# Sample states of a hybrid decoder layer: the first decay factor taken out of the scores, the outgoing prompt state in two slots, the values' rows in half tiles, and HGRN2's factors copied at level 64

## The chip, the cores and the metric

The kernel runs on one core of a Trainium2 chip. The core has a matrix engine (TensorE, PE in the profile; its weight loads are PEld), a vector engine (VectorE, DVE), a scalar engine (ScalarE, ACT), a general engine (GpSimd, POOL) and a sync engine (SyncE, SP) that issues most DMA transfers. Each engine works through its own instructions in order. The metric is the device time of one execution in microseconds (us), lower is better.

## The reference, cut to what matters

One inference step of one decoder layer for 256 + 16 prompt tokens and 8 sample tokens: a half-step FFN, a mixer, a second half-step FFN, with 2048 channels. The mixer is one projection of 2048 to 20480 channels, then 8 heads of retention (256 x 256 states) and 16 heads of HGRN2 (128 x 128 states) side by side, a gated merge and one output projection. A sample token updates a stored state of its own in each head and reads it:

```python
# retention, one sample token (C = 1): gamma is a constant of the head
S_new = gamma * S + k^T v                 # k_dec = k
o = (q k^T) v + (gamma * q) S             # q_dec = q * gamma
# HGRN2, one sample token: f is a vector of 128 factors, k = 1 - f
S_new = f[:, None] * S + k^T v
o = (q k^T) v + (q * f) S
...
def decoder_layer(x, pos, s_ret, s_hg, prompt, ...):
    x = layer_norm(ALPHA * x + 0.5 * swiglu(x, f1_g, f1_u, f1_d), ln1_g, ln1_b)
    m, s_ret, s_hg = token_mixer(x, pos, s_ret, s_hg, prompt, w_in, lb, hg_norm_g, w_out)
    x = layer_norm(ALPHA * x + m, ln2_g, ln2_b)
    x = layer_norm(ALPHA * x + 0.5 * swiglu(x, f2_g, f2_u, f2_d), ln3_g, ln3_b)
    return x, s_ret, s_hg
```

The outputs are the tokens and all states, those of the prompt and those of the samples (8 samples x 8 heads x 256 x 256 and 8 x 16 x 128 x 128 numbers).

## The kernel before, in words

All tokens stand side by side in the free dimension (280 columns, 264 where the meta tokens aren't needed), channels on the partitions. Every dense product is made in three passes, with the operands split into a high and a low part: `xh` by `whi`, `xl` by `whi`, `xh` by `wlo`. The weights stream through in units of 512 KB (eight 128 x 128 blocks): SP loads `raw` (L184), ACT casts it to `whi` (L187), DVE subtracts to get `wlo` (L188), PE does 24 matmuls (L217). There are three buffers of each.

PE's order is written out by hand in the program. The projection runs head by head (`pj_q_r`, `pj_k_r`, `pj_v_r`, `pj_q_h`, `pj_f`, `pj_i_h`; then the gates `pj_g_r`, `pj_a_r`, `pj_g_h`, `pj_a_h` of the head before), and the mixers are generators that are advanced by a few steps after each slice of the projection: a `yield n` in them says after how many such steps they go on. The order on ACT, DVE, POOL and SP is made by the tile scheduler from this program; on the chip it is fixed.

`mix_ret` is one retention head `u`. It splits keys and values (`ks`, `vs`), computes the scores of the prompt (`psc`) and multiplies them with a decay table into `dtab`'s tile (`scr`), and computes the outgoing prompt state in two halves `psr`, each copied by ACT into a tile with the tag `sro` (L1051) and written out (`out_srp`, L1052). The sample states come in four tiles `smr` (128 x 4 x 256: one half of the key channels, four samples each; L988). ACT multiplies a whole tile by the head's constant, which POOL has put in a small tile `gam` (L1062, L1067); then DVE adds key times values' row for each sample (L1070). For that the values' rows of the samples are written to a scratch (`vrd`, L720) and read back spread over all partitions into `vbr` (L1038). `gam` shares the one slot of the tag `sro` with the outgoing state:

```python
gam = tmp("sro", (P, 1))
nc.gpsimd.memset(gam, GAMMA[u])
```

The new states go out (`out_srs`, L1073), and 32 small matmuls `pqr` read them (L1084), after the prompt's four small matmuls at L1025. `vbr` is one buffer of 4 x 256 numbers a partition, so its second spread (samples 4 to 7) waits for the last update of samples 0 to 3.

`mix_hg` is the two HGRN2 heads of the same `u`. It works through levels of doubling length (2, 4, ... 64, 128): `scale_k` and `scale_q` multiply keys and queries in place by a level's decay, from the tile of the tag `T2`, `T4`, ... `T64`. Its sample states `smh` (16 heads x 8 samples) are scaled one sample at a time by ACT, with the sample's factors `fk[:, 0]` (L906), and updated by DVE (L907), then written out (L910) and read by the matmuls `pq`.

Of the kernel before, what the change touches and what calls it, by code (L numbers as in the profile page):

```python
# [13 lines left out]
AF = mybir.ActivationFunctionType  # L14
ALU = mybir.AluOpType
# [3 lines left out]
P = 128  # L19
# [4 lines left out]
NMETA, SEQ, NS = 16, 256, 8  # L24
LP = NMETA + SEQ
# [28 lines left out]
GAMMA = [1.0 - 2.0 ** (-5.0 - h) for h in range(HR)]  # L54
# [73 lines left out]
def trunk(ctx: ExitStack, tc: tile.TileContext, A, O):  # L128
    nc = tc.nc
# [416 lines left out]
    with tc.tile_pool(name="yp", bufs=1) as yp:  # L546
# [7 lines left out]
        with tc.tile_pool(name="mp", bufs=1) as mp:  # L554

            rows = {n: (r if isinstance(r, list) else [r]) for n, r in {
# [3 lines left out]
            }.items()}  # L560

            def tmp(name, shape=(P, T), bufs=1, dt=F32, tag=None):
                if name in rows:
                    rows[name] = rows[name][1:] + rows[name][:1]
                    return rp.tile(list(shape), dt, tag=rows[name][-1], name=name)
                return mp.tile(list(shape), dt, tag=tag or name, name=name, bufs=bufs)
# [166 lines left out]
            def mix_hg(u, f, k, q, v):  # L733
# [11 lines left out]
                fk = tmp("fk", (P, 2, 2, NS))  # L745
# [4 lines left out]
                sms, vbs = [], []  # L750
# [78 lines left out]
                vrow = []  # L829
                for h in range(2):  # L830
# [4 lines left out]
                    x = pt[:64, 2 * P : 3 * P]  # L835
# [24 lines left out]
                for s in LEVELS[MASKED:]:  # L860
                    pl = mx_bank("pl")
                    for h in range(2):
                        for b in range(2):
                            k0, q0, o = NMETA + b * P, b * P, (2 * h + b) * s
                            if s == 64:
                                j = 64 * b
# [24 lines left out]
                Tt = Ts[2 * LEVELS[-1]]  # L891
                on = tmp("on_h", (P, 2, TL), bufs=2)
                on_h[u] = on
                kts = []
                for h in range(2):
                    kt = tmp("kth", (P, 2, P), bufs=2)
                    kts.append(kt)
                    pt = mx_bank("ptk")
                    for b, (t0, n) in enumerate(((NMETA, P), (NMETA + P, P), (0, NMETA))):
                        nc.tensor.transpose(pt[:n, b * P : (b + 1) * P], K[:, h, t0 : t0 + n], ident)  # L900
                    nc.scalar.copy(kt, pt[:, : 2 * P].rearrange("p (b f) -> p b f", b=2))
                    upper_upper_lower(km[:, h, :], pt[:NMETA, 2 * P : 3 * P])

                    vb, sm = vbs[h], sms[h]
                    for b in range(NS):
                        nc.scalar.activation(sm[:, b, :], sm[:, b, :], AF.Copy, scale=fk[:, 0, h, b : b + 1])  # L906
                        nc.vector.scalar_tensor_tensor(  # L907
                            out=sm[:, b, :], in0=vb[:, b, :], scalar=fk[:, 1, h, b : b + 1], in1=sm[:, b, :],
                            op0=ALU.mult, op1=ALU.add)
                    nc.sync.dma_start(O["sgs"][2 * u + h], sm)  # L910
                    yield 2
# [3 lines left out]
                for h in range(2):  # L915
# [7 lines left out]
                    for b in range(2):  # L923
                        nc.vector.scalar_tensor_tensor(
                            out=S[:, b + 1, :], in0=S[:, b, :], scalar=Tt[:, h, b : b + 1],
                            in1=pst[:, (b + 1) * P : (b + 2) * P], op0=ALU.mult, op1=ALU.add)
# [3 lines left out]
                for h in range(2):  # L930
                    for b in range(NS):
                        j = 32 * (b % 4)
# [45 lines left out]
            def mix_ret(u, q, k, v):  # L978
# [4 lines left out]
                sms = []  # L983
# [11 lines left out]
                for c in range(2):  # L995
# [12 lines left out]
                    for b, (t0, n) in enumerate(BLOCKS):  # L1008
                        x, g = pt[:n, b * P : (b + 1) * P], dec[:n, b, u : u + 1]
                        his = [ks[:, 0, b, f]] if b < 2 else [ks2[third[0], c, :], ks2[third[1], c, :]]  # L1010
                        for hi in his:
                            nc.scalar.activation(hi, x, AF.Copy, scale=g)
                        nc.vector.scalar_tensor_tensor(
                            out=(ks[:, 1, b, f] if b < 2 else ks2[third[2], c, :]), in0=x, scalar=g,
                            in1=his[0].bitcast(F32), op0=ALU.mult, op1=ALU.subtract)
# [15 lines left out]
                c2 = SCORES[2][0]  # L1031
                mul(scr[:, :c2], psc[:, :c2], dt[:, :c2])
                scrs = [scr[:, SCORES[0][0] : SCORES[1][0]], scr[:, SCORES[1][0] : c2], sc2]
                vbs = []

                def spread(e):
                    vbs.append(tmp("vbr", (P, 4, 256)))
                    nc.sync.dma_start(vbs[e], vrow[4 * e : 4 * e + 4, :].partition_broadcast(P))  # L1038

                spread(0)  # L1040
                yield 4

                for c in range(2):
# [14 lines left out]
                centre(vlast.unsqueeze(1))  # L1058
                upper_lower_upper(vs2.rearrange("p c f -> p (c f)"), vlast)

                gam = tmp("sro", (P, 1))
                nc.gpsimd.memset(gam, GAMMA[u])  # L1062
                for e in range(2):
                    vb = vbs[e]
                    for c in range(2):
                        sm = sms[2 * e + c]
                        nc.scalar.activation(sm, sm, AF.Copy, scale=gam)  # L1067
                        for j in range(4):
                            t = LP + 4 * e + j
                            nc.vector.scalar_tensor_tensor(  # L1070
                                out=sm[:, j, :], in0=vb[:, j, :], scalar=k[:, c, t : t + 1], in1=sm[:, j, :],
                                op0=ALU.mult, op1=ALU.add)
                        nc.sync.dma_start(O["srs"][u, c, :, 4 * e : 4 * e + 4, :], sm)  # L1073
                    if e == 0:
                        spread(1)
                    yield 1 + 5 * (1 - e)
                yield 15 + 2 * calm
                pq = mx_bank("pqr")
# [171 lines left out]
```

## Time and profile before

| | |
|---|---|
| median of 3 runs | 2607.2 us (2603.62 to 2609.99) |
| the profiled execution | 2608.29 us, of which 2606.2 us are the profile's span |
| granted PE clock in it | 0.997 of full speed |
| first FFN | 0 to about 790 us |
| the eight heads | about 790 to 1800 us |
| output projection and second FFN | about 1800 us to the end |
| w_in loads | 320 transfers of 512 KB, 4.5 us from issue to landing |
| sample states in / out (retention) | 32 / 32 transfers of 512 KB, 4.7 / 4.7 us |
| spreads of the values' rows | 16 transfers of 512 KB, 4.1 us |

A profile shows one execution. "A <- B" in a list of waits means that A sat idle until B was done. A row of a timeline has the start, the length, the engine, the line of the program, the operation, what it writes and reads, and in brackets the idle time of the engine just before it and what ended that. SPq is SP's queue of DMA issues: a row there is the issue, not the transfer.

### The profile page before, as it was taken

Reading aid. Unit: us, or ns where it says so; the run is one execution under the profiler, and the core shown is the slowest. Engines: PE = TensorE matmul, PEld = TensorE weight load, DVE = VectorE, ACT = ScalarE, POOL = GpSimd, SP = SyncE. Lnnn points to the kernel's source line nnn. Section 1 sums busy time; section 2 is a strip of 40 time slices with the busy share of each in tenths; the row PEclk is TensorE's granted clock in tenths of the full one; section 3 lists DMA queues with packets and bytes.
Section 4 is the critical chain, followed back from the end, with each engine's and each line's share of the span. In section 5 each row is a group of like instructions: output and inputs, shape, how many; then the busy total and the mean of one; then the engine's idle time right before and its main releaser. Section 6 shows DMA issues by size and latency. Waiting matters only on the chain.

```text
span 2606.2 us, 56106 instructions
## 1 busy us (share of the span) xinstructions
PE 2580.9 (99%) x23400; PEld 2546.5 (98%) x23400; DVE 1703.7 (65%) x2859; ACT 1375.4 (53%) x2160; POOL 13.7 (1%) x62
## 2 busy tenths in 40 slices
PE   9999999999999989999999999999999999999999
PEld 9999999999999889999999999999999999999998
DVE  6444454565579777777777777776995555556555
ACT  5444444444456566666666666665564444444444
POOL 0000000000000000000000000000000000000000
PEclk9999999999999999999999999999999999999999
DMA  7555555555566675767676767676656666666664
GB/s 240 184 183 185 186 185 182 184 186 185 182 200 223 216 269 183 265 207 260 210 258 210 256 206 263 203 235 194 193 187 201 195 195 195 195 197 193 197 197 147
DMA packets 154591, 536.25 MB, mean 206 GB/s; under 512 B 17696, under 2 KB 25696, under 8 KB 154336
## 3 DMA queue, kind: packets, MB, share of 16 engines
q1 hardware_dynamic: 154048, 532.37, 63.0%
q8 instruction: 183, 3.00, 0.5%
q14 instruction: 72, 0.59, 0.1%
q10 hardware_dynamic: 288, 0.29, 0.0%
HBM read 501.99 MB, written 30.61 MB: 204 GB/s over the span
## 4 chain that ended last, share of the span: by engine, by line
PE 92%; DVE 4%; DMA 2%; ACT 1%; issue 1%; SPq 0%; POOL 0%; ACTq 0%; POOLq 0%; DVEq 0%
PE up L217 35%; PE dn L217 18%; PE pj_f L217 4%; PE pj_q_h L217 3%; PE wo L217 3%; PE pj_k_r L217 3%; PE pj_v_r L217 3%; PE pj_g_r L217 3%; PE pj_i_h L217 3%; PE pj_q_r L217 3%; PE pj_a_r L217 3%; PE pj_g_h L217 3%; PE pj_a_h L217 3%; DVE wlo L188 2%; DMA vbr<-vrd 1%; PE pqr L1084 1%
## 5 line engine op out<-in xcount | busy, mean ns | idle before, releaser
L188 DVE TENSOR_TENSOR wlo<-raw,whi 128x1024 fp32r<-128x1024 f32 (+1 forms) x869 | 1062.4, 1223 | 748.6 <-ACT whi L187 745.4
L187 ACT CAST whi<-raw 128x1024 fp32r<-128x1024 f32 (+1 forms) x870 | 905.3, 1042 | 911.4 <-PE up L217 413.1
L217 PE MATMUL up<-xh,wlo 128*128 128x280 f32 (+1 forms) x2624 | 726.0, 280 | 1.3 <-DVE wlo L188 1.3
L217 PE MATMUL up<-xh,whi 128*128 128x280 f32 (+1 forms) x2624 | 725.7, 280 | 1.0 <-ACT whi L187 1.0
L217 PE MATMUL up<-xl,whi 128*128 128x280 f32 (+1 forms) x2624 | 725.4, 279 | 0.0
L217 PEld LDWEIGHTS up<-xh,wlo 128*128 128x128 f32 x2624 | 492.5, 189 | 2.3 <-DVE wlo L188 2.3
L217 PEld LDWEIGHTS up<-xh,whi 128*128 128x128 f32 x2624 | 492.6, 189 | 1.3 <-ACT whi L187 1.2
L217 PEld LDWEIGHTS up<-xl,whi 128*128 128x128 f32 x2624 | 492.6, 189 | 0.0
L217 PE MATMUL dn<-hh,whi 128*128 128x280 f32 (+1 forms) x1376 | 384.7, 280 | 0.0
L217 PE MATMUL dn<-hh,wlo 128*128 128x280 f32 (+1 forms) x1376 | 384.3, 279 | 0.0
L217 PE MATMUL dn<-hl,whi 128*128 128x280 f32 (+1 forms) x1376 | 384.3, 279 | 0.0
L217 PEld LDWEIGHTS dn<-hh,whi 128*128 128x128 f32 x1376 | 260.1, 189 | 0.1
L217 PEld LDWEIGHTS dn<-hl,whi 128*128 128x128 f32 x1376 | 260.1, 189 | 0.1
L217 PEld LDWEIGHTS dn<-hh,wlo 128*128 128x128 f32 x1376 | 260.1, 189 | 0.0
L217 PE MATMUL pj_g_r<-xh,whi 128*128 128x264 f32 x256 | 76.8, 300 | 0.0
L217 PE MATMUL pj_g_h<-xh,whi 128*128 128x264 f32 x256 | 73.7, 288 | 0.0
L217 PE MATMUL pj_k_r<-xh,whi 128*128 128x280 f32 x256 | 73.7, 288 | 0.0
L217 PE MATMUL pj_v_r<-xh,whi 128*128 128x280 f32 x256 | 73.5, 287 | 0.0
L217 PE MATMUL pj_v_r<-xh,wlo 128*128 128x280 f32 x256 | 72.4, 283 | 0.3 <-DVE wlo L188 0.3
L217 PE MATMUL pj_k_r<-xh,wlo 128*128 128x280 f32 x256 | 72.5, 283 | 0.0
L217 PE MATMUL pj_k_r<-xl,whi 128*128 128x280 f32 x256 | 72.3, 283 | 0.0
L217 PE MATMUL pj_v_r<-xl,whi 128*128 128x280 f32 x256 | 72.3, 283 | 0.0
(393 smaller groups left out, 5235.6 us busy)
## 6 DMA issues: line engine op xcount, KB each, us to landing
raw<-in_w_up SPq DMA_DIRECT2D x343, 512.0 KB, 4.2
raw<-in_w_in SPq DMA_DIRECT2D x320, 512.0 KB, 4.5
raw<-in_w_dn SPq DMA_DIRECT2D x172, 512.0 KB, 3.4
smr<-in_sr SPq DMA_DIRECT2D x32, 512.0 KB, 4.7
out_srs<-smr SPq DMA_DIRECT2D x32, 512.0 KB, 4.7
raw<-in_w_out SPq DMA_DIRECT2D x32, 512.0 KB, 3.5
smh<-in_sg SPq DMA_DIRECT2D x16, 512.0 KB, 4.7
vbr<-vrd SPq DMA_DIRECT2D x16, 512.0 KB, 4.1
```

Of the source, the lines that this page charges most:

```text
L187: nc.scalar.copy(hi[:, j:jn, :], raw[:, j:jn, :])
L188: nc.vector.tensor_tensor(out=lo[:, j0:j1, :], in0=raw[:, j0:j1, :], in1=hi[:, j0:j1, :].bitcast(F32), op=ALU.subtract)
L217: nc.tensor.matmul(o, w, t, start=start, stop=stop)
L1084: nc.tensor.matmul(pq[32 * j : 32 * j + 32, :256], qdr[:, c, 32 * b : 32 * b + 32], sms[2 * e + c][:, j, :], start=e + c == 0, stop=e + c ...
```

## The change

Four edits. The tag `sro` gets a second slot. The constant of the first two state tiles is made by POOL out of the scores' tile (minimum and maximum with the same constant, so the value is the constant and only the dependence is on the scores), in a tile of its own; the constant of the last two is a memset as before. The values' rows come in halves of two samples, in two buffers, four spreads a head, and both tiles of a pair of halves are scaled ahead of the pair's eight updates. In HGRN2, POOL copies the factors `fk[:, 0]` into a tile of the tag `T64`, and ACT scales by the copy. That tile can be written only when level 64's `scale_k` and `scale_q` have read theirs.

```diff
-                "sro": "d9", "osh": "d10", ...
+                "sro": ["d9", "d16"], "osh": "d10", ...
@@ mix_hg
+                fs = tmp("fs", (P, 2, NS), tag="T64")
+                nc.gpsimd.tensor_copy(fs, fk[:, 0])
...
-                        nc.scalar.activation(sm[:, b, :], sm[:, b, :], AF.Copy, scale=fk[:, 0, h, b : b + 1])
+                        nc.scalar.activation(sm[:, b, :], sm[:, b, :], AF.Copy, scale=fs[:, h, b : b + 1])
@@ mix_ret, after the scores
+                gams = [tmp("gam", (P, 1))]
+                nc.gpsimd.tensor_scalar(
+                    out=gams[0], in0=scr[:, 0:1], scalar1=GAMMA[u], scalar2=GAMMA[u], op0=ALU.min, op1=ALU.max)
                 vbs = []
-                def spread(e):
-                    vbs.append(tmp("vbr", (P, 4, 256)))
-                    nc.sync.dma_start(vbs[e], vrow[4 * e : 4 * e + 4, :].partition_broadcast(P))
+                def spread(i):
+                    if i < 4:
+                        vbs.append(tmp("vbr", (P, 2, 256), bufs=2))
+                        nc.sync.dma_start(vbs[i], vrow[2 * i : 2 * i + 2, :].partition_broadcast(P))
                 spread(0)
+                spread(1)
@@ mix_ret, after the prompt state
-                gam = tmp("sro", (P, 1))
-                nc.gpsimd.memset(gam, GAMMA[u])
+                gams.append(tmp("sro", (P, 1)))
+                nc.gpsimd.memset(gams[1], GAMMA[u])
                 for e in range(2):
-                    vb = vbs[e]
+                    ss = sms[2 * e : 2 * e + 2]
+                    for sm in ss:
+                        nc.scalar.activation(sm, sm, AF.Copy, scale=gams[e])
+                    for i in (2 * e, 2 * e + 1):
+                        for c in range(2):
+                            for b in (2 * i, 2 * i + 1):
+                                x, t = ss[c][:, b - 4 * e, :], LP + b
+                                nc.vector.scalar_tensor_tensor(
+                                    out=x, in0=vbs[i][:, b - 2 * i, :], scalar=k[:, c, t : t + 1], in1=x, op0=ALU.mult, op1=ALU.add)
+                        spread(i + 2)
                     for c in range(2):
-                        sm = sms[2 * e + c]
-                        nc.scalar.activation(sm, sm, AF.Copy, scale=gam)
-                        for j in range(4):
-                            t = LP + 4 * e + j
-                            nc.vector.scalar_tensor_tensor(
-                                out=sm[:, j, :], in0=vb[:, j, :], scalar=k[:, c, t : t + 1], in1=sm[:, j, :],
-                                op0=ALU.mult, op1=ALU.add)
-                        nc.sync.dma_start(O["srs"][u, c, :, 4 * e : 4 * e + 4, :], sm)
-                    if e == 0:
-                        spread(1)
+                        nc.sync.dma_start(O["srs"][u, c, :, 4 * e : 4 * e + 4, :], ss[c])
                     yield 1 + 5 * (1 - e)
```

PE's order is the same in both. The other engines' orders change in the mixer. Buffer numbers differ between the two programs; a unit of weights that is `raw_10169` before is `raw_10175` after.

SP in head 0, where the second spread stands before:

```order
L184 DMA raw_10169<-in_w_in 128x1024
L910 DMA out_sgs<-smh 128x1024
L184 DMA raw_10199<-in_w_in 128x1024
L1073 DMA out_srs<-smr 128x1024
L184 DMA raw_10269<-in_w_in 128x1024
L184 DMA raw_10304<-in_w_in 128x1024
L1073 DMA out_srs<-smr 128x1024
L184 DMA raw_10385<-in_w_in 128x1024
L1038 DMA vbr<-vrd 128x1024
```

and the same place after, from the issues of the first two halves on:

```order
L1044 DMA vbr<-vrd 128x512
L184 DMA raw_10126<-in_w_in 128x1024
L1059 DMA out_srp<-sro 128x256
L990 DMA smr<-in_sr 128x1024
L1059 DMA out_srp<-sro 128x256
L990 DMA smr<-in_sr 128x1024
L184 DMA raw_10175<-in_w_in 128x1024
L1044 DMA vbr<-vrd 128x512 x2
L184 DMA raw_10205<-in_w_in 128x1024
```

The last two spreads stand straight behind the load that is `raw_10169` before, ahead of four weight loads and three writes of states that the second spread stood behind.

DVE in head 3, between scores and `pqr`, before (`wlo_15140` is a unit of the gates, `km`, `gt` and `y` are short steps of the mixers):

```order
L188 TENSOR_TENSOR wlo_15068<-raw_15066,whi_15067 128x8x128
L239 TENSOR_TENSOR gt<-gt,gs 128x264
L254 TENSOR_TENSOR km<-ptk,km 16x128
L239 TENSOR_TENSOR y<-gt,on_r 128x264
L188 TENSOR_TENSOR wlo_15098<-raw_15096,whi_15097 128x8x128
L1070 SCALAR_TENSOR_TENSOR smr<-vbr,k_r,smr 128x256 x6
L188 TENSOR_TENSOR wlo_15140<-raw_15138,whi_15139 128x8x128
L1070 SCALAR_TENSOR_TENSOR smr<-vbr,k_r,smr 128x256 x2
```

and after, between the same two units (now `wlo_15100` and `wlo_15172`):

```order
L188 TENSOR_TENSOR wlo_15100<-raw_15098,whi_15099 128x8x128
L239 TENSOR_TENSOR gt<-gt,gs 128x264
L254 TENSOR_TENSOR vs_8641<-vt_8636,vs_8641 24x256
L239 TENSOR_TENSOR y<-gt,on_r 128x264
L254 TENSOR_TENSOR km<-ptk,km 16x128
L909 SCALAR_TENSOR_TENSOR smh<-vbh,fk,smh 128x128 x4
L188 TENSOR_TENSOR wlo_15130<-raw_15128,whi_15129 128x8x128
L909 SCALAR_TENSOR_TENSOR smh<-vbh,fk,smh 128x128 x3
L254 TENSOR_TENSOR km<-ptk,km 16x128
L909 SCALAR_TENSOR_TENSOR smh<-vbh,fk,smh 128x128 x5
L188 TENSOR_TENSOR wlo_15172<-raw_15170,whi_15171 128x8x128
```

HGRN2's updates stand here now. The first eight `smr` updates have moved up: two single ones ahead of `wlo_15058`, six between it and `wlo_15100`, with `vt`, one `gt` and one `smh` among them.

DVE in head 7, around the keys of the prompt state (`ks`), before:

```order
L1013 SCALAR_TENSOR_TENSOR ks_8640<-pt,dec,ks_8640 24x128
L1013 SCALAR_TENSOR_TENSOR ks<-pt,dec,ks 128x128
L254 TENSOR_TENSOR km<-ptk,km 16x128
L239 TENSOR_TENSOR dtab<-psc,dtab 128x400
L1013 SCALAR_TENSOR_TENSOR ks<-pt,dec,ks 128x128
```

and after:

```order
L1015 SCALAR_TENSOR_TENSOR ks<-pt,dec,ks 128x128
L254 TENSOR_TENSOR km<-ptk,km 16x128
L909 SCALAR_TENSOR_TENSOR smh<-vbh,fk,smh 128x128 x2
L1015 SCALAR_TENSOR_TENSOR ks<-pt,dec,ks 128x128
L909 SCALAR_TENSOR_TENSOR smh<-vbh,fk,smh 128x128 x5
L239 TENSOR_TENSOR dtab<-psc,dtab 128x400
L188 TENSOR_TENSOR wlo_22358<-raw_22356,whi_22357 128x8x128
L1015 SCALAR_TENSOR_TENSOR ks_8640<-pt,dec,ks_8640 24x128
```

Ten of the `smh` updates, seven of them in these rows, now stand between the first and the last of the six `ks`; before, all stood ahead of them.

On POOL each head's memset is joined by the factor out of the scores (its tile appears by the name of the scores' tile, `dtab`) and the copy `fs`; in head 0 a row `L1037 ISA`, an instruction that names a code library, stands ahead of the first factor and behind `ends`, two copies at the head of each head.

2 rows, old and new, of the table rows are left out of this document.

## The prediction

> **What bounds the kernel now.** I read the page first, then the waits of the matrix engine (PE), then the windows of the mixer, and last the timelines around the waits.
>
> ```profile
> span 2606.2 us, 56106 instructions
> PE 2580.9 (99%) x23400; PEld 2546.5 (98%) x23400; DVE 1703.7 (65%) x2859; ACT 1375.4 (53%) x2160; POOL 13.7 (1%) x62
> ```
>
> PE is busy for 2580.9 of 2606.2 us, so 25.3 us are open in the whole kernel. An edit that leaves PE's work alone, as this one does, can gain those 25.3 us and what a slowed clock adds to busy time, no more. Who is waited for (columns: us in total, times, longest):
>
> ```profile
> PE pqr L1084 <- DVE smr L1070: 9.9, 3, 5.2
> PE pj_q_h L217 <- DVE wlo L188: 1.0, 1, 1.0
> PE pj_g_h L217 <- DVE wlo L188: 1.0, 1, 1.0
> PE psr L1049 <- DVE ks L1013: 0.6, 1, 0.6
> ```
>
> The largest wait is the retention sample output (`pqr`) waiting for the vector engine (DVE) to finish the updated states `smr`: 9.9 us in three waits, where there are eight heads. The windows show where it is not (columns: window, length, busy time and count of PE, PEld, DVE, ACT, POOL, then granted PE clock, DMA share, GB/s):
>
> ```profile
> 862.00:864.00 2.00, 1.58 (x7) 0.73 (x8) 2.00 (x6) 0.00 (x0) 0.00 (x0) 0.50 1.04 424
> 1107.00:1752.00 645.00, 644.40 (x6358) 629.48 (x6357) 492.09 (x993) 415.38 (x777) 7.16 (x26) 1.00 0.70 231
> 1200.00:1220.00 20.00, 20.00 (x184) 19.84 (x184) 14.45 (x26) 14.63 (x25) 0.10 (x1) 1.00 0.88 299
> ```
>
> From 1107 to 1752 us (the rest of head 2 up to head 7) PE is open for 0.60 us: nothing can be gained there, only lost. The waits stand in heads 0 and 1. PE at head 0:
>
> ```profile
> 857.10 0.24 PE L1025 MATMUL pqr<-q_r,k_r 128*16 128x16 f32 x3
> ...
> 862.42 3.83 PE L1084 MATMUL pqr<-smr,qdr 128*32 128x256 f32 x16 [4.17 <-DVE smr L1070]
> 866.18 0.60 PE L217 MATMUL pj_i_h<-xh,whi 128*128 128x280 f32 x1
> ...
> 867.68 0.28 PE L217 MATMUL pj_i_h<-xh,whi 128*128 128x280 f32 x1
> 867.80 0.28 PE L217 MATMUL pj_i_h<-xl,whi 128*128 128x280 f32 x1
> ```
>
> and what it waited for, on DVE and on the sync engine's DMA queue (SP):
>
> ```profile
> 848.18 0.48 DVE L1070 SCALAR_TENSOR_TENSOR smr<-vbr,k_r,smr 128x256 f32<-128x256 f32 x1
> 861.88 3.25 DVE L1070 SCALAR_TENSOR_TENSOR smr<-vbr,k_r,smr 128x256 f32<-128x256 f32 x8 [2.97 <-DMA vbr<-vrd]
> 854.30 0.33 SPq L184 DMA_DIRECT2D raw<-in_w_in  x1
> 854.68 0.43 SPq L1038 DMA_DIRECT2D vbr<-vrd  x1
> ```
>
> DVE was done with the first four tokens at 848.66. The second spread of the values' rows (`vbr`) could then have started, since the one buffer was free, but SP issued it at 854.68, behind a weight load, and DVE got it at 861.88. Head 1 has the same, and before it a stall of its own kind:
>
> ```profile
> 952.67 0.10 POOL L1062 MEMSET sro<- 128x1 f32 x1 [79.48 <-DMA out_srp<-sro]
> 952.80 1.15 ACT L1067 ACTIVATE smr<-smr,sro 128x1024 f32<-128x1024 f32 x1 [5.23 <-POOL sro L1062]
> 956.45 0.38 PE L217 MATMUL pj_g_h<-xh,wlo 128*128 128x264 f32 x1 [1.02 <-DVE wlo L188]
> 963.89 0.43 SPq L1038 DMA_DIRECT2D vbr<-vrd  x1
> 965.78 0.24 PE L1025 MATMUL pqr<-q_r,k_r 128*16 128x16 f32 x3
> 972.16 1.06 PE L1084 MATMUL pqr<-smr,qdr 128*32 128x256 f32 x2 [5.24 <-DVE smr L1070]
> 976.97 0.39 PE L217 MATMUL pj_f<-xh,whi 128*128 128x280 f32 x1
> ```
>
> The decay factor lives in the one slot of the outgoing prompt state, so its memset on POOL waits until that state has been written out; ACT waits 5.23 us for the factor, and the first scaled state, DVE's work on it and the second spread all start late. Head 2 is the undisturbed pass:
>
> ```profile
> 1090.88 0.24 PE L1025 MATMUL pqr<-q_r,k_r 128*16 128x16 f32 x3
> 1093.59 0.38 PE L217 MATMUL pj_g_r<-xh,whi 128*128 128x264 f32 x1
> ```
>
> **The change part by part: what goes.** From the first `pqr` matmul to the next projection matmul head 0 takes 866.18 − 857.10 = 9.08 us, head 1 takes 976.97 − 965.78 = 11.19, head 2 takes 1093.59 − 1090.88 = 2.71. The excess over head 2 is 6.37 + 8.48 = 14.85 us; it holds the waits and the matmuls at half clock behind them (0.50 in the window 862 to 864). Six more projection matmuls run slowly after head 0's pass: 867.68 − 866.18 = 1.50 us for six that take 6 × 0.12 = 0.72 at the pitch of the last two rows, so 0.8. The two waits for `wlo` of 1.0 us each fall in heads 0 and 1, behind an ACT that waits for the factor. Together 14.85 + 0.8 + 2.0 = 17.6 us.
>
> Does the change take all of it? The first factor now comes out of the scores, long before the outgoing state; the second is a memset in a slot whose previous state went out one copy earlier. In the new order the third and fourth half spreads of head 0 stand on SP four weight loads and three state writes ahead of where the second spread stood, and each waits only for the half before last to be used. I take all 17.6 as gone, except a small rest: in head 0 the last three state updates stand behind one more `wlo` (1.2 us each by the rows below), and I take a third of that, 0.4, for each of heads 0 and 1: 0.8, bounds 0 and 2.4.
>
> **What is given back in heads 2 to 6.** There the edit at level 64 holds HGRN2's state work back. Rows of head 3:
>
> ```profile
> 1178.89 2.40 DVE L907 SCALAR_TENSOR_TENSOR smh<-vbh,fk,smh 128x128 f32<-128x128 f32 x8 [1.26 <-ACT smh L906]
> 1195.38 0.33 SPq L1038 DMA_DIRECT2D vbr<-vrd  x1
> 1205.32 1.23 DVE L188 TENSOR_TENSOR wlo<-raw,whi 128x1024 fp32r<-128x1024 f32 x1 [0.24 <-ACT whi L187]
> 1206.46 2.46 DVE L1070 SCALAR_TENSOR_TENSOR smr<-vbr,k_r,smr 128x256 f32<-128x256 f32 x6
> 1208.84 1.22 DVE L188 TENSOR_TENSOR wlo<-raw,whi 128x1024 fp32r<-128x1024 f32 x1
> 1213.33 0.42 DVE L239 TENSOR_TENSOR gt<-gs,pj_g_h 128x264 f32<-128x264 f32 x1
> 1213.67 1.22 DVE L188 TENSOR_TENSOR wlo<-raw,whi 128x1024 fp32r<-128x1024 f32 x1
> 1211.16 0.28 PE L217 MATMUL pj_a_h<-xh,wlo 128*128 128x264 f32 x1
> 1211.50 0.28 PE L217 MATMUL pj_g_r<-xh,wlo 128*128 128x264 f32 x1
> ```
>
> The sixteen `smh` updates (2.40 / 8 = 0.30 us each), of which the last eight ended at 1181.3, move into the stretch after the scores, where the eight early `smr` updates (2.38 / 6 = 0.40 each) now begin as well. The unit that PE starts on at 1211.3 needs its `wlo` at 1211.50; DVE's row at 1208.84 ended at 1210.06, 1.44 us ahead, the tightest of the head. In the new order this stands on DVE ahead of it, from the first `smr` update on: 8 × 0.40 = 3.2, 3 × `wlo` at a pitch of 1.14 = 3.4, seven short ones at the pitch of 0.34 that the row at 1213.33 has = 2.4, and 13 × 0.30 = 3.9, then the `wlo` itself, 1.2: 14.1 us. When does the first update start? The spread is issued at 1195.38. A 512 KB spread lands in 4.1 us (longest wait and median below); half of it I put at 3.3, between half of that, 2.05, and all of it, so DVE starts at 1198.7 and the `wlo` is done at 1212.8: 1.3 us late if nothing else gives. One of the three earlier `wlo` is late by a little too, and each unit on PE shifts the next need by what was lost, so I take 1.0 us a head; bounds 0 (the spread lands at half, and DVE starts 1.25 us earlier) and 2.5 (it takes all of 4.1, and one more short instruction falls in). Five heads: 5.0 us, bounds 0 and 12.5.
>
> ```profile
> vbr<-vrd SPq DMA_DIRECT2D x16, 512.0 KB, 4.1
> ```
>
> The Trainium skill, in "SBUF — State Buffer", section "The DMA setup-cost knee", speaks against half tiles: every transfer pays a fixed 2 us or so, and the time is about that plus the bytes over 436 GB/s. By it, as an estimate, a half lands at 2.6 us and two of them pay 5.2 where the whole pays 3.2; the trace has 4.1 for the whole, 0.9 more, and with 2.6 for a half the loss per head would be about 0.3 instead of 1.0.
>
> HGRN2's states (2 × 512 KB) are also written out later, in the stretch 1200 to 1220 with a DMA share of 0.88 already; what they displace are weight loads, whose buffers wait for PE rather than for the bus, and I cost it at nothing; if that cover is gone it is in the 2.5 above.
>
> **Head 7.** Ten `smh` updates now stand on DVE between the `ks` of the prompt state, for whose last one PE already waits 0.6 us: 10 × 0.30 = 3.0 us if no gap of DVE takes them, 0 if all fall into gaps. I take the middle, 1.5; bounds −0.6 (the old wait gone) and 3.0.
>
> **POOL.** The factor out of the scores and the copy of HGRN2's factors are new work on POOL, and a code-loading instruction stands ahead of the first factor. The nearest row beside the memset's:
>
> ```profile
> 799.67 1.48 POOL L737 COPY ends<-v 128x32 f32<-128x32 f32 x1 [51.84 <-DVE v L411]
> ```
>
> One small instruction costs between 0.10 (the memset) and 1.48 us; POOL is busy 1% and both ends lie inside the wait for the spread. The load stands behind an instruction at 801 us, and the factor is wanted 30 us later: nothing on the path.
>
> **Sum.** −17.6 + 0.8 + 5.0 + 1.5 = −10.3 us. The profiled execution took 2606.2 us of span and 2608.3 in all, 1.1 over the median of 2607.2; taken off the median this gives 2596.9 us.
>
> **The rivals.** (a) *Nothing is given back*: the half spreads land early and the gaps of DVE (14.45 of 20 us busy in the window 1200 to 1220) take the moved work. −17.6 us, 2589.6. For it: that idle share; against: the 14.1 us of unbroken work. Chance 0.15. (b) *The stalls move*: heads 2 to 6 lose 3.0 us each, a little above my upper bound, because ACT, with sixteen scalings ahead of the casts, is late as well as DVE. −17.6 + 0.8 + 15.0 + 1.5 = −0.3, 2606.9. For it: PE's slack of 1.44 us. Chance 0.13. (c) *Slower, by two queues that hold each other*: DVE now has `smr` updates ahead of a `wlo`, these wait for a spread, the spread stands on SP behind a weight load, and that load waits for a buffer which this `wlo`'s unit frees. Heads 0 and 1 show the price, 5.24 us at most. In heads 2 to 6 that is 26.2: −17.6 + 0.8 + 26.2 + 1.5 = +10.9, 2618.1. It decides from about 4.6 us a head, that is, a half landing some 5 us later than I put it. Against: in head 3 the first spread is issued at 1195.38 without delay. Chance 0.14. (d) *The code load falls on the path*: it is fetched only when the first factor is asked for, at the scores of head 0, and ACT, with casts behind that scaling, stops. The nearest row is ACT's wait of 5.23 in head 1, which cost PE 1.02 at once and some of the 5.24 later; with 4.2, head 0's stall, the sum is −6.1, 2601.1. Chance 0.08.
>
> The Trainium skill, "GPSIMD Engine Reference", section "2.1 Instruction dispatch", says that the first call to freshly loaded code pays about 6 us without an instruction to show for it; that is the mechanism of (d), and no run here shows it yet.
>
> **How the numbers follow.** The forecast with its own bounds has 0.50, (a) 0.15, (b) 0.13, (c) 0.14, (d) 0.08. A measurement can tell 0.3%, 7.8 us, from no change. Forecast and (a) are faster by more: 0.65. (b) and (d) lie within: 0.21. (c) is slower: 0.14. By its own bounds the forecast runs from −18.2 (2589.0) to +0.3 (2607.5); the range takes in these, (a), (b) and (d), with about a microsecond beyond each end, 2588 to 2608, and leaves out (c).
>
> **What would show it.** Right: `pqr` no longer waits for `smr` in heads 0 and 1 and the pass takes about 2.7 us there; small waits of projections for `wlo`, about 1 us a head, between 1107 and 1752; PE open there for some 5 us instead of 0.6. Wrong: (a) no such waits; (b) 3 us of them a head, some for `whi`; (c) DVE waiting for `vbr` with projections waiting behind it; (d) one wait of ACT for `gam` in head 0. A `pqr` that still waits in heads 0 and 1 would overturn the first term.

## The result, and the profile after

The changed kernel takes 2597.35 us (median of 9 runs, 2593.9 to 2600.48), the kernel before 2604.35 (9 runs, 2603.62 to 2609.99). The ratio is 0.9969, 95% interval 0.9961 to 0.9978: 7 to 8 us less, about 0.3%. The profiled execution of after took 2593.9 us and that of before 2608.29, so this pair shows 14.4 us where the medians differ by 7.0; 1.5 us of it lie in the first FFN, which is the same in both (head 0's first `pj_k_r` matmul starts at 790.4 instead of 791.9). A second profile of after (2598.25 us, `again` below) is used beside it. Two of the nine executions of one kernel below, h23, took 6950 and 12133 us; its interval is taken without them.

The waits of PE in after:

```profile
PE pl L872 <- DVE Q L239: 2.4, 1, 2.4
PE por L729 <- ACT yh L224: 1.8, 1, 1.8
PE psr L1056 <- DVE ks L1015: 1.5, 1, 1.5
PE ptk L902 <- DVE K L239: 1.4, 1, 1.4
PE pj_i_h L217 <- DVE wlo L188: 1.3, 1, 1.3
PE pj_q_h L217 <- DVE wlo L188: 1.1, 1, 1.1
...
PE ptk L902 <- DVE km L254: 0.6, 1, 0.6
```

`pqr`, 9.9 us before, is gone from the list. Five waits that before did not have stand in its place, and one, of `psr`, has grown. The timeline of PE shows the retention pass of head 0 and the new waits:

```profile
847.51 0.39 PE L217 MATMUL pj_i_h<-xh,wlo 128*128 128x280 f32 x1 [1.31 <-DVE wlo L188]
852.09 0.29 PE L872 MATMUL pl<-Q,K 128*32 128x32 f32 x6 [2.40 <-DVE Q L239]
858.76 0.24 PE L1027 MATMUL pqr<-q_r,k_r 128*16 128x16 f32 x3
...
858.88 1.89 PE L1091 MATMUL pqr<-smr,qdr 128*32 128x256 f32 x29
860.70 0.39 PE L217 MATMUL pj_i_h<-xh,whi 128*128 128x280 f32 x1
...
953.77 0.33 PE L902 MATMUL ptk<-ident,K 128*128 128x128 f32 x1 [1.45 <-DVE K L239]
969.09 0.30 PE L729 MATMUL por<-ident,osr 128*128 128x128 f32 x1 [1.75 <-ACT yh L224]
```

The pass takes 860.70 − 858.76 = 1.94 us, and it takes 1.94 us in all eight heads of after. The prediction took head 2 of before, 2.71 us, for undisturbed. It was not. Head 6 of before, in its timeline, is the clean one:

```profile
1607.59 0.24 PE L1025 MATMUL pqr<-q_r,k_r 128*16 128x16 f32 x3
...
1607.70 1.89 PE L1084 MATMUL pqr<-smr,qdr 128*32 128x256 f32 x29
1609.52 0.38 PE L217 MATMUL pj_g_r<-xh,whi 128*128 128x264 f32 x1
```

and head 3 of before, PE and DVE, shows what slows the others:

```profile
1219.91 0.24 PE L1025 MATMUL pqr<-q_r,k_r 128*16 128x16 f32 x3
...
1220.03 2.85 PE L1084 MATMUL pqr<-smr,qdr 128*32 128x256 f32 x29
1222.81 0.38 PE L217 MATMUL pj_g_r<-xh,whi 128*128 128x264 f32 x1
1220.14 2.06 DVE L1070 SCALAR_TENSOR_TENSOR smr<-vbr,k_r,smr 128x256 f32<-128x256 f32 x5
```

DVE is still making the last five updates while PE reads the states. The 29 matmuls spread over 2.85 us instead of 1.89; each wait is short, the row merges them, and no list of waits names them. So "PE is open for 0.60 us of 645" was true of the columns and wrong as a statement of what could be gained.

### The profile page after: what moved, and what is told of

Same layout as the page of the kernel before. It is cut to its first block, busy times and chain, and to the rows that moved or that the text cites. A ratio compares the mean times of both kernels' runs of the same rounds, so it can differ in the third digit from the quotient of the medians.

```text
span 2592.1 us, 56133 instructions
## 1 busy us (share of the span) xinstructions
PE 2570.6 (99%) x23400; PEld 2543.1 (98%) x23400; DVE 1703.8 (66%) x2859; ACT 1374.9 (53%) x2160; POOL 19.6 (1%) x78
## 4 chain that ended last, share of the span: by engine, by line
PE 59%; DVE 1%; ACT 1%; issue 0%; POOL 0%; DVEq 0%; ACTq 0%; POOLq 0%
PE up L217 17%; PE dn L217 9%; PE wo L217 3%; PE pj_g_r L217 3%; PE pj_g_h L217 3%; PE pj_a_h L217 3%; PE pj_k_r L217 3%; PE pj_a_r L217 3%; PE pj_v_r L217 3%; PE pj_q_r L217 2%; PE pj_i_h L217 2%; PE pj_f L217 2%; PE pj_q_h L217 2%; DVE wlo L188 0%; PE pqr L1091 0%; PE por L1106 0%
```

## The experiments

Twelve kernels, each compared with the kernel before. The last three columns are read from each one's profile: from the first `pj_k_r` matmul of head 0 to that of head 2, from there to that of head 7, and from there to the first `wo` matmul. What lies ahead of them takes 789.9 to 791.9 us, what lies behind, up to the end of the last matmul, 797.2 to 797.3. Two profiles of the same kernel (after, `again`) differ by 1.1, 2.6 and 0.5 in these columns, so smaller steps in them are not read.

| kernel | edits | median us | ratio, 95% interval | heads 0, 1 | heads 2 to 6 | head 7 |
|---|---|---|---|---|---|---|
| before | none | 2604.4 to 2605.4 | 1 | 237.6 | 646.0 | 127.4 |
| after | 1 2 3 4 | 2597.35 | 0.9969 (0.9961 to 0.9978) | 225.4 | 643.3 | 129.7 |
| again | 1 2 3 4 | 2596.74 | 0.9968 (0.9956 to 0.9981) | 226.5 | 645.9 | 129.2 |
| no4 | 1 2 3 | 2598.28 | 0.9976 (0.9966 to 0.9985) | 226.7 | 646.1 | 127.9 |
| only12 | 1 2 | 2608.95 | 1.0013 (1.0004 to 1.0023) | 227.9 | 656.1 | 129.6 |
| only3 | 3 | 2587.59 | 0.9933 (0.9920 to 0.9945) | 219.9 | 643.8 | 127.4 |
| h34 | 3 4 | 2596.20 | 0.9966 (0.9954 to 0.9979) | 224.1 | 645.7 | 129.4 |
| h13 | 1 3 | 2590.65 | 0.9944 (0.9931 to 0.9956) | 225.3 | 642.4 | 126.9 |
| h23 | 2 3 | 2599.39 | 0.9974 (0.9964 to 0.9985) | 230.9 | 645.4 | 127.9 |
| hso | 1 3, factor from `so` | 2588.61 | 0.9941 (0.9929 to 0.9954) | 226.2 | 646.9 | 126.9 |
| order1 | loop of 3, whole tile | 2593.48 | 0.9959 (0.9946 to 0.9973) | 224.3 | 642.3 | 130.4 |
| quart | 3 in quarters | 2590.67 | 0.9952 (0.9939 to 0.9964) | 224.5 | 643.0 | 127.5 |
| only4 | 4 | 2616.16 | 1.0048 (1.0035 to 1.0060) | 228.9 | 655.8 | 134.3 |
| no4ld | 1 2 3, loads earlier | 2598.26 | 0.9975 (0.9966 to 0.9985) | 229.0 | 644.7 | 128.6 |

(The profile of hso is of its longest execution, 2595.3 us.)

A wait of PE can cost more than its length, since matmuls behind it can run at half clock. In the windows of `again` and then of after (columns as in the prediction; the clock is the number ahead of the last two):

```profile
854.00:857.00 3.00, 3.00 (x15) 3.00 (x15) 2.60 (x7) 1.05 (x1) 0.00 (x0) 0.50 0.89 309
```

```profile
854.00:857.00 3.00, 3.00 (x28) 3.00 (x27) 1.96 (x5) 1.19 (x2) 0.00 (x0) 1.00 0.98 322
```

PE does 15 matmuls at a granted clock of 0.50 and 28 at 1.00. In `again` it had waited 2.17 and 2.41 us just before, in after 1.31 and 2.40. By the clock in the traces such a stretch lasts 3.4 us, or twice that, so it costs some 1.7 us, or 3.4, as an estimate, where PE is busy throughout. Heads 0 and 1 have none in after, only3 and order1; one in again, no4, only12, quart and only4; two in h34, h13, h23 and no4ld; a double one in hso; and two double ones in before. Head 2 has one in hso, head 7 one in order1 and in only4. The lists of waits leave this out; it is part of the differences in these columns.

**again**: the same kernel.

> The changed kernel once more, for a second profile beside the first, which was taken in its fastest execution. Theory (the retention pass no longer waits for its states in any head, about 20 us; new waits in heads 0, 1 and 7 take back about 8): eight passes of 1.94 us again, the time 6 to 10 us under the kernel before. Rival (the cover of 0.06 us that two units of each of heads 3 to 6 have left breaks in other executions): the same passes, but waits of 0.2 us or more for wlo in those heads, in all 3 us or more, which the first profile does not have.

The passes are 1.94 us again, the ratio is the same. The waits for `wlo` in heads 2 to 6, from 1015 to 1664 us, which the first profile does not have at all:

```profile
PE pj_g_r L217 <- DVE wlo L188: 1.1, 2, 0.9
PE pj_q_h L217 <- DVE wlo L188: 0.4, 1, 0.4
PE pj_g_h L217 <- DVE wlo L188: 0.3, 1, 0.3
```

1.8 us: in between the two theories. The largest, 0.9 in head 3, is not a matter of thin cover: DVE stood for the third half spread with that `wlo` behind it.

```profile
1202.08 1.67 DVE L1078 SCALAR_TENSOR_TENSOR smr<-vbr,k_r,smr 128x256 f32<-128x256 f32 x4 [1.42 <-DMA vbr<-vrd]
1203.67 1.22 DVE L188 TENSOR_TENSOR wlo<-raw,whi 128x1024 fp32r<-128x1024 f32 x1
```

Whether such waits are why the runs of after spread over 6.6 us is not shown; those of before spread over 6.4.

**no4**: the change without its fourth edit.

```diff
-                fs = tmp("fs", (P, 2, NS), tag="T64")
-                nc.gpsimd.tensor_copy(fs, fk[:, 0])
...
-                        ... scale=fs[:, h, b : b + 1])
+                        ... scale=fk[:, 0, h, b : b + 1])
```

> The change without its fourth edit: HGRN2's states are scaled by the factors themselves, so they are updated early again. Theory (first three edits make the gain, the fourth costs in heads 0, 1 and 7 what it crowds): passes of about 1.94 us in all heads, no wait of PE for psr above 0.6 us in head 7, 8 to 14 us under the kernel before. Rival (the fourth edit clears DVE for the retention states and is needed for the gain): the passes of heads 2 to 6 take 2.5 us or more as before, and the time is within 4 us of the kernel before.

The passes are 1.94 us, so the fourth edit is not needed for them, but the time is that of after, 6 us under before, below the range I gave. In head 7 the wait for `psr` did not go either: it is 1.6 us, and head 1 has one of 0.7. Both theories were short of something.

**only12**: the first two edits on the kernel before.

```diff
-                "sro": "d9", ...
+                "sro": ["d9", "d16"], ...
...
+                gams = [tmp("gam", (P, 1))]
+                nc.gpsimd.tensor_scalar(out=gams[0], in0=scr[:, 0:1], scalar1=GAMMA[u], scalar2=GAMMA[u], op0=ALU.min, op1=ALU.max)
...
-                gam = tmp("sro", (P, 1))
-                nc.gpsimd.memset(gam, GAMMA[u])
+                gams.append(tmp("sro", (P, 1)))
+                nc.gpsimd.memset(gams[1], GAMMA[u])
```

> The kernel before with the first two edits alone: two slots for the outgoing state and the first factor out of the scores; the values' rows stay in one whole tile. Theory (the early factor lets the first four samples be done early, so the one buffer is free and the second spread is issued early): pqr waits gone in heads 1 to 6, 5 to 12 us under the kernel before. Rival (the half tiles do it): head 0 and head 1 still wait 3 us or more each for the second spread, 0 to 4 us under.

**only3**: the third edit on the kernel before, one late factor.

```diff
-                    vbs.append(tmp("vbr", (P, 4, 256)))
+                    vbs.append(tmp("vbr", (P, 2, 256), bufs=2))
...
+                    for sm in ss:
+                        nc.scalar.activation(sm, sm, AF.Copy, scale=gam)
+                    for i in (2 * e, 2 * e + 1):
+                        ... (four updates)
+                        spread(i + 2)
```

> The kernel before with the third edit alone: the values' rows in half tiles, two buffers, both tiles scaled first; one factor in the one slot of the outgoing state as before. Theory: the spreads come earlier on SP, so head 0 loses most of its 7 us, but ACT still waits some 5 us for the factor in head 1 and PE for the states behind it: 2 to 6 us under the kernel before. Rival (the half tiles alone make the gain): no pass above 2.2 us, 7 us or more under.

These two turned my theory over. The early factor, which I had as the main part of the gain, makes the kernel 3 to 4 us slower with the second slot and without the halves, and all eight passes still take 2.7 us or more. The half tiles alone gain 17 us, twice what the whole change gains, and their five runs lie within 1.0 us. PE's waits in `only3`:

```profile
PE pl L867 <- DVE Q L239: 1.2, 1, 1.2
PE pj_g_r L217 <- DVE wlo L188: 1.2, 1, 1.2
```

and no other wait of the mixer in its list is above 1.0 us. Which of the other edits takes the gain back was the next question.

**h34**, **h13**, **h23**: the half tiles with one other edit each.

> The third and the fourth edit: half tiles for the values' rows and HGRN2's factors copied at level 64; the factor as before, one slot. Theory now (the half tiles alone make the whole gain; the other edits only take back): passes of 1.94 us, but waits of the output matmuls, ptk and psr come back in heads 0, 1 and 7, in all 2 to 5 us: 12 to 15 us under the kernel before, where the half tiles alone are 17 under. Rival (with the late factor the fourth edit takes updates off the busy stretch ahead of the scores and helps): 17 to 20 us under.

> The first and the third edit: half tiles and two slots for the outgoing state, both factors a memset in a slot. The factor then comes one transfer earlier than with one slot, later than out of the scores. Theory (an early factor lets the scaling of the last two state tiles stand on ACT ahead of casts while their loads are still under way): ACT waits for smr<-in_sr come back, some us in all, and PE waits for wlo behind them: 10 to 15 us under the kernel before. Rival (the second slot only removes the 8.9 us that ACT waits for the factor): 17 us under or more, PE waits below those of the half tiles alone.

> The second and the third edit: half tiles, and the first factor out of the scores, with one slot for the outgoing state. Theory (the first factor out of the scores is what costs): ACT waits for smr<-in_sr of 2 to 4 us in several heads, PE waits for wlo and pl behind them, 5 to 11 us under the kernel before, as with all three edits. Rival (the second slot, which brings the second factor early, is what costs): 15 us under or more.

h34: the fourth edit on top of the halves costs 8.7 us (0.9966 against 0.9933), more than I expected, with the three waits of after, in its list of PE's waits:

```profile
PE por L729 <- ACT yh L224: 1.8, 1, 1.8
PE psr L1053 <- DVE ks L1015: 1.5, 1, 1.5
...
PE ptk L902 <- DVE km L254: 0.6, 1, 0.6
```

None of them is in the list of `only3` in this size, where `psr` has 0.8 in two. And head 2's pass takes 3.41 us, not 1.94. h13: the second slot costs about 3 us; the five runs of each kernel do not overlap, the intervals do. Its reason was not the one I gave, since ACT waits for `smr<-in_sr` only once there, 0.7 us; the loss is in heads 0 and 1 (`ptk` 2.2, `pj_i_h` 2.1, and two stretches at half clock). h23: the factor out of the scores costs 10.7 us on top of the halves, and 11.0 more in heads 0 and 1 of its profile than the halves alone, some 3.4 of it at half clock; with the second slot as well (no4) it is as much. By the medians that is the dearest edit; its interval overlaps that of h34.

**only4**: the fourth edit on the kernel before, the first pair of lines of no4's diff put in.

> The kernel before with the fourth edit alone: HGRN2's factors copied at level 64. Theory (it moves sixteen updates a head into the stretch where DVE has the retention updates, and gives nothing): 2 to 9 us over the kernel before, as the half tiles with it are 9 us over the half tiles without. Rival (it only costs beside the half tiles): within 2 us.

11 to 12.5 us slower, beyond my range. All eight passes are longer than 3.8 us; head 3's:

```profile
1210.77 0.24 PE L1027 MATMUL pqr<-q_r,k_r 128*16 128x16 f32 x3
...
1210.88 4.53 PE L1086 MATMUL pqr<-smr,qdr 128*32 128x256 f32 x29
```

Thirteen HGRN2 updates stand between the scores and the first retention update there and three more ahead of the ninth, so the second spread is issued 5.7 us ahead of the pass (1205.10), where before has 8.6 (1211.28 for 1219.91). Its cost is not a constant: 12.5 us alone, 8.7 with the halves, and nothing that can be told beside all three others (after 0.9969, no4 0.9976), where the retention updates have gone ahead of it.

**hso**: the factor of both pairs made by POOL out of the first half of the outgoing state, ready between the scores and the memset.

```diff
+                    if c == 0:
+                        gams = [tmp("gam", (P, 1))] * 2
+                        nc.gpsimd.tensor_scalar(out=gams[0], in0=so[:, 0:1], scalar1=GAMMA[u], scalar2=GAMMA[u], op0=ALU.min, op1=ALU.max)
                     nc.sync.dma_start(O["srp"][u, c], so)
```

> The half tiles with both factors made by POOL out of the first half of the outgoing prompt state (two slots, a factor tile of its own): a factor that is ready between the scores and the memset. Theory (the earlier the factor, the more casts stand behind a scaling that waits for its load): between the early factor and the late one, 9 to 15 us under the kernel before. Rival (only the dependence on the scores is bad, since DVE then waits for the first half spread with wlo behind): 17 us under or more.

15 to 17 us under before: close to the rival, not to "the earlier the worse". A factor out of the first half costs nothing that can be told beside h13, which has the second slot too, and 2 us beside the halves alone; out of the scores it costs 10.

**order1**, **quart**: the third edit taken apart.

```diff
# order1: the loop of the third edit, the whole tile in one buffer
+                    for sm in ss:
+                        nc.scalar.activation(sm, sm, AF.Copy, scale=gam)
+                    for j in range(4):
+                        for c in range(2):
+                            ... (one update)
+                    if e == 0:
+                        spread(1)
+                    for c in range(2):
+                        nc.sync.dma_start(O["srs"][u, c, :, 4 * e : 4 * e + 4, :], ss[c])
# quart: tiles of one sample
-                        vbs.append(tmp("vbr", (P, 2, 256), bufs=2))
+                        vbs.append(tmp("vbr", (P, 256), bufs=4))
```

> The kernel before with the loop of the third edit only: both state tiles scaled first, updates sample by sample, writes at the end; the values' rows stay whole in one buffer, so the second spread still starts after the eighth update. Theory (what gains is that a half is free after four updates and its next spread is issued then): little, passes of heads 0 and 1 still 7 us or more, within 4 us of the kernel before. Rival (the order of updates and writes makes the gain): 10 us under or more.

> The third edit in quarters: the values' rows in tiles of one sample, four buffers, eight spreads a head of 128 KB; the same memory, the late factor. Theory (the release of a buffer in time is what counts, and two buffers already give it): passes of 1.94 us, 14 to 19 us under the kernel before, no better than halves by more than 2 us. Rival (smaller transfers land so much later, each paying a fixed time, that updates are late): passes above 2.2 us or waits for vbr above 15 us in all, 12 us under or less.

order1 is 10.7 us under before, with the second spread as large and as dependent as before. In its program the spread stands ahead of the writes of the states, and SP in head 0 follows:

```profile
847.45 2.93 SPq L184 DMA_DIRECT2D raw<-in_w_in  x2
850.43 0.42 SPq L1038 DMA_DIRECT2D vbr<-vrd  x1
```

850.43 instead of 854.68. Heads 2 to 7 have passes of 1.94 us; heads 0 and 1 have 5.54 and 3.47. So of the 17 us some 11 come from the order of the loop and 6 from the halves. Which part of that order does it (both scalings first, the updates by sample, or the writes behind the spread) was not taken apart. Quarters are no better than halves: 12.5 to 14 us under. Head 0's `pl` waits 2.8 us instead of 1.2 and its pass takes 3.31 us, which the theory did not have, but DVE waits for `vbr` only 3.8 us in all, so the rival's late transfers do not show either.

**no4ld**: no4 with the loads of the last two state tiles ahead of the second write of the outgoing state.

```diff
+                    if c == 1:
+                        load(1)
                     so = tmp("sro", (P, 256))
...
-                load(1)
```

> The first three edits, with the loads of the last two state tiles issued ahead of the second write of the outgoing state instead of behind it. Theory (with the early factor ACT scales before it copies the outgoing state, so its writes are late on SP, the loads behind them are late, and ACT waits for these with casts behind): ACT waits for smr<-in_sr in heads 2 to 6 shrink from 9.4 us in all to under 5, PE waits of pj_g_r for wlo from 2.7 us to under 1.5: 2 to 3 us faster than with the first three edits alone, so 9 to 10 us under the kernel before. Rival (DVE is late by its own updates, whatever ACT does): the waits of pj_g_r and the time are as with the three edits alone.

ACT in no4 and then in no4ld, its waits from 1100 to 1690 us:

```profile
ACT smr L1071 <- DMA smr<-in_sr: 9.4, 4, 2.9
```

```profile
ACT smr L1072 <- DMA smr<-in_sr: 5.9, 4, 2.0
```

ACT's waits shrank by a third, less than I said, and PE's wait of `pj_g_r` for `wlo` went from 2.7 to 1.0 us, as the theory said. The time did not move (0.9975 against 0.9976): heads 2 to 6 have 1.4 us less in its profile and heads 0 and 1 2.3 more. The chain ACT, cast, `wlo` exists, but loosening it did not change the time. Most of what the early factor costs lies in heads 0 and 1: no4 has 226.7 there and no4ld 229.0, where the halves alone have 219.9.

**Where an early factor costs.** DVE in head 0 of after, and SP's issue of the two halves it waits for:

```profile
840.37 0.90 SPq L1044 DMA_DIRECT2D vbr<-vrd  x2
845.84 0.48 DVE L1078 SCALAR_TENSOR_TENSOR smr<-vbr,k_r,smr 128x256 f32<-128x256 f32 x1 [3.00 <-DMA vbr<-vrd]
846.24 1.22 DVE L188 TENSOR_TENSOR wlo<-raw,whi 128x1024 fp32r<-128x1024 f32 x1
...
851.62 0.42 DVE L239 TENSOR_TENSOR Q<-Q,T 128x256 f32<-128x256 f32 x1
```

and the same in `only3`:

```profile
845.29 0.33 SPq L1039 DMA_DIRECT2D vbr<-vrd  x1
847.45 0.42 DVE L239 TENSOR_TENSOR Q<-Q,T 128x256 f32<-128x256 f32 x1
...
849.47 1.67 DVE L1073 SCALAR_TENSOR_TENSOR smr<-vbr,k_r,smr 128x256 f32<-128x256 f32 x4
```

In after, the factors are ready, so the fifth sample's update stands on DVE ahead of a `wlo` and of HGRN2's `Q`. It comes before its values do: DVE stands for 3.00 us, the `wlo` and `Q` stand behind it, and PE waits 1.31 us for the one and 2.40 for the other. In `only3` the late factor holds that update back; the spread is issued 5 us later, has landed when DVE comes, and `Q` is done 4.2 us earlier. The wait of `pl` on this `Q` is the first factor's: it is 2.2 to 2.4 us in all five profiles that have the halves and the factor out of the scores (after, again, no4, h23, no4ld), and the same row (L872) does not wait in h13, hso and h34. The wait of `pj_i_h` does not need that factor, since those three have it too (1.6 to 2.1). This shows head 0 only. In head 1 of h23 an early update waits for another thing: ACT stands 4.74 us for the second factor, in the one slot, DVE 1.92 for the scaled state, and `ptk` 3.11 for the `K` behind it.

## Why the prediction was right or wrong

The time came within 0.5 us of the forecast and the sign was right, but that closeness is luck, twice over. The forecast was 10.3 us under a median of 2607.2 that three runs gave; nine runs gave 2604.35, and the change is 7.0 under that (5.7 to 10.2 by the interval). And in the sum three terms were wrong by 4 to 6 us and largely cancelled. Against the first profile of after:

| term | predicted | measured |
|---|---|---|
| passes of `pqr` | −14.85 | −20.1 (35.6 − 8 × 1.94; heads 2 to 5 give 3.7 of it, the rest is heads 0 and 1) |
| slow matmuls behind head 0's stall | −0.8 | −0.8 |
| waits for `wlo` in heads 0 and 1 | −2.0 | −1.0; `pj_q_h` still has one, 1.1, one unit earlier |
| rest in heads 0 and 1 | +0.8 | +6.9 (1.31 + 2.40 + 1.45 + 1.75) |
| heads 2 to 6 | +5.0 | +1.0 (3.7 from the passes less the 2.7 of the column), none of it in a listed wait; in the second profile +3.6, of which 1.8 in waits |
| head 7 | +1.5 | +2.3 by the column, 1.5 of it in `psr` (0.6 to 1.5) and `ptk` (0.6); in the second profile +1.8 |

With a wait of 0.5 for `whi` that went too, the column sums to −12.2; the eight heads of the two profiles differ by 12.6, and the other 1.5 of the 14.1 in the spans lie ahead of them. By stretches, heads 0 and 1 were forecast at −16.8 and gave −12.2 (second profile −11.1), heads 2 to 6 at +5.0 and gave −2.7 (−0.1).

**The first term** failed at "head 2 takes 2.71" as the undisturbed pass. The quick check would have been the shortest of the eight, 1.94 in heads 6 and 7.

**The rest in heads 0 and 1** failed at "I take all 17.6 as gone". I followed the wait that goes and costed three late updates, not what else stands on DVE behind an update that comes too early. That is rival (c) in part, by its mechanism: a state update waits for a spread with a `wlo` behind it. I had placed it in heads 2 to 6 and not where the spreads were already late. Of the four waits `pl` comes with the factor out of the scores, `ptk` on `K` with any earlier factor (h13 and hso have it too) and `por` with the fourth edit (h34). The second profile adds a stretch at half clock in head 0, which the sum had at nothing.

**Heads 2 to 6**: the replay had the tight unit 1.3 us late, and no list has a wait for it in either profile (one of the units ahead of it is 0.3 late in head 2 of `again`). In head 3 of after, SP, DVE and PE:

```profile
1178.94 0.33 SPq L1044 DMA_DIRECT2D vbr<-vrd  x1
1182.98 0.48 DVE L1078 SCALAR_TENSOR_TENSOR smr<-vbr,k_r,smr 128x256 f32<-128x256 f32 x1 [0.28 <-ACT smr L1073]
...
1195.81 1.22 DVE L188 TENSOR_TENSOR wlo<-raw,whi 128x1024 fp32r<-128x1024 f32 x1
1197.08 0.38 PE L217 MATMUL pj_g_r<-xh,wlo 128*128 128x264 f32 x1
```

From the first update to the end of that `wlo` it is 14.05 us, as replayed (14.1), and the first update starts 4.0 us after the issue, not 3.3. The step that failed is the time of the issue, which I took from before: it is now 18.1 us ahead of PE's need (1178.94 to 1197.08) and not 16.1 (1195.38 to 1211.50). Why it moved was not taken apart. So the 1.0 us a head went for the wrong reason; the largest wait that did come in these heads, 0.9 in the second profile, is rival (c)'s. The sign that I gave, PE open for some 5 us between 1107 and 1752, failed too: it is 3.3 us in the first profile, all of it in head 7's waits. Rivals (a) and (b) are out by heads 0 and 1, which gave back 6.9, and by heads 2 to 6, which lost 0.2 and 0.7 us a head and not 3.0.

A first half spread takes 4.2 us in head 0 of after (issued at 828.54, DVE goes on at 832.78) and 3.9 in head 2 of `again`; the first whole spreads of heads 2 to 7 before take 3.9 to 4.3. (The 4.1 of the table ahead of the change is the median of these six, the only ones whose landing the profile has; the second spreads took longer, see the end.) By the Trainium skill's "SBUF — State Buffer", section "The DMA setup-cost knee", a half would take about 2.6 us and a whole 3.2, as an estimate. Both measurements, in a stretch where other transfers run, stand above these figures.

**Rival (d)** is out. POOL's first factor in after:

```profile
829.28 0.19 POOL L1037 TENSOR_SCALAR gam<-dtab 128x1 f32<-128x1 f32 x1 [29.46 <-DVE cen L977]
```

0.19 us, and POOL was idle for 29.46 before it, released by DVE. ACT waits for `gam` 0.7 us in the whole kernel. If the 6 us that the Trainium skill, "GPSIMD Engine Reference", section "2.1 Instruction dispatch", gives for a first call were paid, they lie in that idle time; no run here shows them.

**Which edit does what** I had not asked in the prediction, and there the profile had more to say than I read: the other three edits together take back 10 of the 17 us that the third gains. The third alone, 2587.59 us, 0.67% under before (0.55 to 0.80), beats both kernels. Not tried: why the halves' rest of 2.4 us (`pl` in head 0, `pj_g_r` in head 2) stays, and more buffers for the state tiles.

## What to carry to other kernels

When a repeated stretch is stalled in some rounds, measure the others against the shortest round, not against a typical one: short waits inside a merged row of busy matmuls are named by no list of waits. Making an input early is no gain by itself on an engine with a fixed order: an instruction that is allowed to stand earlier stands there waiting for its other input, with everything queued behind it; ask of each thing that comes early what else its reader needs, and when that lands. And try the parts of a change one by one, since their costs do not add.

## What was not expected of the hardware

Halving a transfer did not always halve, or even shorten, the time from its issue until DVE, which waits for it, goes on. The first spread of a head took 3.9 to 4.2 us as a half against 3.9 to 4.3 as a whole. The second spread of a head took 5.9 to 7.7 us before; the third half, in its place, took 5.5 to 8.3 in after and 3.5 to 4.8 in `only3`. What else was under way then was not taken apart. Halving it still paid, by some 6 us on top of order1.

And the same kernel had a stretch at half clock in head 0 in `again`, behind waits of 2.17 and 2.41 us, and none in after, behind 1.31 and 2.40.
